# Who issues the transfers of a block inversion: from the SP queue to POOL

## The chip, the cores and the metric

The kernel runs on one core of a Trainium2 chip. The metric is the device time of one execution in microseconds (us), lower is better; it is given as the median of several runs. One further execution is taken with the hardware profiler, and it has a time of its own.

## The reference

One inference step of a two-layer trunk for a prompt of 512 tokens and eight sample tokens with a past of 1024. Layer 0 mixes by a gated DeltaNet, layer 1 by dilated sliding-window attention; each is followed by a squared-ReLU MLP. Everything is float32. What matters here is the prompt's part of the gated DeltaNet: 16 value heads, each evaluated in chunks, where each chunk needs the inverse of a unit lower triangular matrix:

```python
kb = k * beta[..., None]
a_strict = jnp.where(strict, jnp.einsum('bhnid,bhnjd->bhnij', kb, k) * decay, 0.0)
t_inv = lax.linalg.triangular_solve(eye + a_strict, ...,
                                    left_side=True, lower=True, unit_diagonal=True)
u = t_inv @ (v * beta[..., None])
w = t_inv @ (kb * jnp.exp(gc)[..., None])
```

The results are then carried through a scan over the chunks. The outputs are the tokens' new activations, the new states, and the caches with a row appended.

## The kernel before

The program runs four stages one after the other: `gdn` (the gated DeltaNet), `mlp`, `dsw` (the attention) and `mlp` again. Tokens lie along the free dimension (512 of the prompt and 8 samples), features along the 128 partitions. A projection is three float32r matmuls per 128 input features (L164 to L166): weights and activations are split into a high and a low part, ScalarE making the high part (L130) and VectorE the low one (L131). Each weight block comes by a DMA of 512 KB on the SP queue (L145) into one of three buffers, and with each of them goes one copy of old cache rows from DRAM to DRAM (L97).

`gdn` works on eight pairs of value heads, numbered 0 to 7 here. In the loop of L914 the steps of pair p are interleaved with those of pair p + 1, and a scheduler, which lays out the program against a model of its own, decides the order of instructions on each engine from priorities. The order on an engine is fixed then: an engine, the SP queue and POOL each take their instructions strictly one after the other, and one that waits holds back all that stand behind it. For the pair p + 1 the steps are:

- `key`, `decay`: the decay products E (eight tiles u of 128 x 128, four chunks by two heads), made on VectorE, the last of them by L603.
- `invert`: the four 32 x 32 diagonal blocks of each of the eight tiles go out to a DRAM scratch D1 with four transfers (L629, 256 rows of 128 bytes each), and come in again as Ft with one (L632), which puts block (b, u) on partition 32q + 8b + u, four times over. So 32 blocks can be inverted at once by POOL, in 31 steps of two instructions (L638, L641) on a tile Uo; the four copies share out the rows of the result. Uo goes out to the scratch D2 with one transfer (L642, 1024 rows of 128 bytes), and comes in as the diagonal blocks of Uf with four (L646). In the profile both scratches are named D, and Uo and Uf, parts of one tile, are named held.
- `query`, `attend`: the q.k products, multiplied into ET on VectorE (L618) and masked on POOL (L619).
- `merge`: the diagonal blocks are combined to the inverse of the whole 128 x 128 tile. It begins on VectorE with three transposes (L653, L654, L655), which wait for Uf, and on TensorE with L660.
- `values`, `scan`, `gates`, `sample`, `out`, `out_proj`: the rest of a pair. In `sample`, the eight sample states S are brought up to date: a row Du goes to DRAM (L834) and is spread to all partitions as ub (L838), POOL multiplies (L839) and adds (L842), and S goes out (L843). In `out`, a rsqrt (L215 to L221), a scaling of the output (L866) and transposes on TensorE (L871).

`invert` and `merge` run at high priority. All transfers of the program are issued by the SP queue. Where a line below says "SP", it is that queue.

Of the kernel before, what the change touches and what calls it, by code (L numbers as in the profile page):

```python
# [366 lines left out]
def gdn(K, l, done):  # L367


    nc, I, O, tc = K.nc, K.I, K.O, K.tc  # L370
# [5 lines left out]
    with ExitStack() as ctx:  # L376
# [155 lines left out]
        class Pair:  # L532
# [88 lines left out]
            @urgent  # L621
            def invert(self):

                E = self.E
                D1 = K.dp.tile([4, U, 32, 32], F32, tag="D1", name="D1")
                D2 = K.dp.tile([4, U, 32, 32], F32, tag="D2", name="D2")
                for b in range(4):
                    s = slice(32 * b, 32 * b + 32)
                    nc.sync.dma_start(D1[b].rearrange("u i j -> i u j"), E[s, :, s])  # L629

                Ft = K.tile(gp, [P, 32, 32], F32, tag="Ft", name="Ft")
                nc.sync.dma_start(Ft, D1.rearrange("b u i j -> (b u) (i j)")[None].to_broadcast([4, 32, 1024]))  # L632
                Uo = part(f"Uo{self.p % 2}", 32)
                tc.keep_in_program_order(nc.gpsimd.tensor_copy(Uo, eyeU))
                tmp = K.tile(gp, [P, 8, 32], F32, tag="fs", name="fs")
                for j in range(31):
                    n, m = 31 - j, j // 4 + 1
                    nc.gpsimd.tensor_tensor(  # L638
                        tmp[:, :m, :n], Ft[:, None, j + 1 :, j].to_broadcast([P, m, n]), Uo[:, :m, j : j + 1].to_broadcast([P, m, n]), ALU.mult
                    )  # L640
                    nc.gpsimd.tensor_tensor(Uo[:, :m, j + 1 :], Uo[:, :m, j + 1 :], tmp[:, :m, :n], ALU.add)  # L641
                nc.sync.dma_start(D2.rearrange("b u (m q) j -> q (b u) m j", q=4), Uo)  # L642
                Uf = self.Uf = Ufs[self.p % len(Ufs)]
                for b in range(4):
                    s = slice(32 * b, 32 * b + 32)
                    nc.sync.dma_start(Uf[s, :, s], D2[b].rearrange("u m j -> m u j"))  # L646

            @urgent
            def merge(self):
# [761 lines left out]
```

## Time and profile before

| what | value |
| --- | --- |
| median of three runs | 2148.9 us (2146.82 to 2150.51) |
| the profiled execution | 2152.49 us |
| its span, first to last instruction | 2150.7 us |
| its mean granted TensorE clock | 0.954 |
| busy: TensorE, VectorE, ScalarE, POOL | 92%, 61%, 41%, 23% |
| DMA issues of one inversion | 10 (4 + 1 + 1 + 4), 8 inversions |

How to read the lines: PE is TensorE, PEld its weight loads, DVE is VectorE, ACT is ScalarE, POOL is GpSimd, SPq the SP queue. L603 is line 603 of the kernel. `E<-kk,base,ET` names the tile written and the tiles read. A timeline line gives the start in us from the span's start, the duration in us, the engine, the line, the operation and its tiles, how many in a row were merged (x4), and in square brackets how long the engine had been idle before and what ended that. A line of waits gives who waited for whom, the total in us, how often, and the longest. A line of the page's groups gives count, busy us, mean ns of one, and the idle time before. For a DMA issue the time is that of writing the transfer's orders, not that of the data. In the windows view a line gives start and end, length, busy us and instruction count of PE, PEld, DVE, ACT and POOL, the granted TensorE clock, the share of the 16 DMA engines that was busy, and GB/s.

### The profile page before, as it was taken

The page shows a single profiled execution, that of the slowest core. Times are in us where ns is not written, and L with a number is a line of the kernel's source. Part 1 is how long each engine was busy: PE and PEld are TensorE (multiplying, and loading weights), DVE is VectorE, ACT ScalarE, POOL GpSimd, SP SyncE. Part 2 cuts the span into 40 slices and gives each one's busy share as a digit, 9 for nine tenths or more (in the row PEclk, how much of TensorE's full clock was granted, in tenths as well). Part 3 has the DMA queues.
Part 4 walks back from the last instruction along what each step waited for, and adds up shares of the span by engine and source line. Part 5 has one row for each costly group of instructions (what it writes and reads, how often), then busy time and mean ns, then how long its engine had stood idle before and what let it go on. Part 6 is the DMA issues. An engine that isn't in the chain of part 4 may idle for free. (4 is left out here: it accounts for less than half of the span.)

```text
span 2150.7 us, 41729 instructions
## 1 busy us (share of the span) xinstructions
PE 1972.8 (92%) x16436; PEld 1937.4 (90%) x16436; DVE 1319.7 (61%) x3301; ACT 892.5 (41%) x2391; POOL 500.4 (23%) x749
## 2 busy tenths in 40 slices
PE   8959867977968789999999999999999989999998
PEld 7858867977968689999999999999999989999998
DVE  4746766956956575454454667666766784454444
ACT  4525433444434352323244545554555443233231
POOL 1162334444344230000001223322332340000000
PEclk8979988989989789999999999999999999999999
DMA  5534554746844538766765774453454333333332
GB/s 139 101 88 134 145 134 135 225 142 167 250 136 134 190 113 281 253 232 230 251 232 204 240 235 131 119 149 99 119 136 133 114 96 89 98 89 91 97 89 70
DMA packets 416277, 328.55 MB, mean 153 GB/s; under 512 B 48408, under 2 KB 404568, under 8 KB 413896
## 3 DMA queue, kind: packets, MB, share of 16 engines
q1 hardware_dynamic: 416080, 325.88, 50.4%
q8 instruction: 129, 2.11, 0.4%
q14 instruction: 68, 0.56, 0.1%
HBM read 302.19 MB, written 132.83 MB: 202 GB/s over the span
## 5 line engine op out<-in xcount | busy, mean ns | idle before, releaser
L164 PE MATMUL mm<-split,whi 128*128 128x260 f32 (+1 forms) x2960 | 861.7, 291 | 22.0 <-DVE base L848 17.4
L166 PE MATMUL mm<-split,wlo 128*128 128x260 f32 (+1 forms) x2960 | 849.1, 287 | 20.3 <-DVE wlo L131 20.3
L165 PE MATMUL mm<-split,whi 128*128 128x260 f32 (+1 forms) x2960 | 846.5, 286 | 1.1 <-DVE split L178 1.1
L164 PEld LDWEIGHTS mm<-split,whi 128*128 128x128 f32 (+1 forms) x2960 | 564.2, 191 | 24.5 <-DVE base L848 17.5
L166 PEld LDWEIGHTS mm<-split,wlo 128*128 128x128 f32 (+1 forms) x2960 | 563.1, 190 | 23.3 <-DVE wlo L131 22.5
L165 PEld LDWEIGHTS mm<-split,whi 128*128 128x128 f32 (+1 forms) x2960 | 564.3, 191 | 2.1 <-DVE split L178 1.5
L130 ACT CAST whi<-raw 128x1024 fp32r<-128x1024 f32 (+1 forms) x273 | 285.4, 1045 | 503.5 <-PE mm L165 484.2
L131 DVE TENSOR_TENSOR wlo<-raw,whi 128x1024 fp32r<-128x1024 f32 (+1 forms) x273 | 336.5, 1233 | 196.9 <-ACT whi L130 188.0
L166 PE MATMUL mm<-hh,wlo 128*128 128x260 f32 x1024 | 289.1, 283 | 0.0
L165 PE MATMUL mm<-hl,whi 128*128 128x260 f32 x1024 | 288.4, 282 | 0.0
L164 PE MATMUL mm<-hh,whi 128*128 128x260 f32 x1024 | 287.9, 282 | 0.0
L165 PEld LDWEIGHTS mm<-hl,whi 128*128 128x128 f32 x1024 | 192.7, 188 | 0.0
L166 PEld LDWEIGHTS mm<-hh,wlo 128*128 128x128 f32 x1024 | 192.6, 188 | 0.0
L164 PEld LDWEIGHTS mm<-hh,whi 128*128 128x128 f32 x1024 | 192.3, 188 | 0.0
L346 DVE TENSOR_TENSOR t<-mm,bc 128x260 f32<-128x260 f32 x128 | 54.8, 428 | 153.1 <-PE mm L166 153.1
L190 POOL TENSOR_TENSOR acc<-acc,sq 128x260 f32<-128x260 f32 x42 | 37.0, 889 | 380.3 <-ACT sq L189 379.9
L638 POOL TENSOR_TENSOR fs<-Ft,held 128x60 f32<-128x60 f32 (+24 forms) x248 | 90.3, 364 | 112.1 <-DMA Ft<-D 93.4
L130 ACT CAST hh<-q 128x260 fp32r<-128x260 f32 x128 | 52.5, 410 | 121.6 <-DVE q L333 121.6
L641 POOL TENSOR_TENSOR held<-held,fs 128x60 f32<-128x60 f32 (+24 forms) x248 | 90.4, 364 | 19.4
L131 DVE TENSOR_TENSOR hl<-q,hh 128x260 fp32r<-128x260 f32 x128 | 54.9, 429 | 57.1 <-ACT hh L130 57.1
L164 PE MATMUL mm<-onh,whi 128*128 128x260 f32 x256 | 85.2, 336 | 2.8 <-DVE ET L618 2.2
L839 POOL TENSOR_TENSOR ub<-ub,base 128x1024 f32<-128x1024 f32 x16 | 32.7, 2044 | 216.7 <-DMA ub<-Du 201.6
(378 smaller groups left out, 3273.9 us busy)
## 6 DMA issues: line engine op xcount, KB each, us to landing
out_dram<-in_cache_kv_w_dram SPq DMA_DIRECT2D x112, 832.0 KB
raw<-in_dsw_w_in_dram SPq DMA_DIRECT2D x72, 512.0 KB
raw<-in_mlp_w_up_dram SPq DMA_DIRECT2D x64, 512.0 KB
raw<-in_mlp_w_down_dram SPq DMA_DIRECT2D x64, 512.0 KB
raw<-in_gdn_w_in_dram SPq DMA_DIRECT2D x48, 512.0 KB
S<-in_state_gdn_dram SPq DMA_DIRECT2D x16, 512.0 KB
raw<-in_gdn_w_out_dram SPq DMA_DIRECT2D x16, 512.0 KB
ub<-Du SPq DMA_DIRECT2D x16, 512.0 KB
```

The costliest lines, as they stand in the source:

```text
L130: nc.scalar.copy(hi, src)
L131: nc.vector.tensor_tensor(lo, src, hi.bitcast(F32), ALU.subtract)
L164: nc.tensor.matmul(ps[:m], lhsT=w[0][:, k, :m], rhs=xh[:, s], start=k == 0, stop=False)
L165: nc.tensor.matmul(ps[:m], lhsT=w[0][:, k, :m], rhs=xl[:, s], start=False, stop=False)
L166: nc.tensor.matmul(ps[:m], lhsT=w[1][:, k, :m], rhs=xh[:, s], start=False, stop=k == nk - 1)
L190: nc.gpsimd.tensor_tensor(acc[:, s], acc[:, s], t, ALU.add)
L346: nc.vector.tensor_tensor(t, ps, r2[:, s], ALU.mult)
L638: nc.gpsimd.tensor_tensor(tmp[:, :m, :n], Ft[:, None, j + 1 :, j].to_broadcast([P, m, n]), Uo[:, :m, j : j + 1].to_broadcast([P, m, n]), A ...
L641: nc.gpsimd.tensor_tensor(Uo[:, :m, j + 1 :], Uo[:, :m, j + 1 :], tmp[:, :m, :n], ALU.add)
L839: nc.gpsimd.tensor_tensor(ub, ub, kqs[:, :, 0:1].to_broadcast([P, NS, P]), ALU.mult)
```

## The change

Ten `dma_start` calls per inversion (in four statements, two of them in loops of four) go from `nc.sync` to `nc.gpsimd`: POOL writes their orders and they stand in POOL's own order of instructions. Source, target and shape of each stay as they were.

```diff
                 for b in range(4):
                     s = slice(32 * b, 32 * b + 32)
-                    nc.sync.dma_start(D1[b].rearrange("u i j -> i u j"), E[s, :, s])
+                    nc.gpsimd.dma_start(D1[b].rearrange("u i j -> i u j"), E[s, :, s])
...
-                nc.sync.dma_start(Ft, D1.rearrange("b u i j -> (b u) (i j)")[None].to_broadcast([4, 32, 1024]))
+                nc.gpsimd.dma_start(Ft, D1.rearrange("b u i j -> (b u) (i j)")[None].to_broadcast([4, 32, 1024]))
...
-                nc.sync.dma_start(D2.rearrange("b u (m q) j -> q (b u) m j", q=4), Uo)
+                nc.gpsimd.dma_start(D2.rearrange("b u (m q) j -> q (b u) m j", q=4), Uo)
...
                 for b in range(4):
                     s = slice(32 * b, 32 * b + 32)
-                    nc.sync.dma_start(Uf[s, :, s], D2[b].rearrange("u m j -> m u j"))
+                    nc.gpsimd.dma_start(Uf[s, :, s], D2[b].rearrange("u m j -> m u j"))
```

No other line differs, but the scheduler lays out all engines anew. The excerpts of POOL's and VectorE's order, before and after, stand in the prediction beside the terms that rest on them.

## The prediction

> **What bounds the kernel now.** I read the page first, then the waits of TensorE, VectorE and the SP queue, then one inversion in order of time. The page's opening lines, and its slices, where each digit is a fortieth of the span (53.8 us):
>
> ```profile
> span 2150.7 us, 41729 instructions
> PE 1972.8 (92%) x16436; PEld 1937.4 (90%) x16436; DVE 1319.7 (61%) x3301; ACT 892.5 (41%) x2391; POOL 500.4 (23%) x749
> ...
> PE   8959867977968789999999999999999989999998
> ...
> PEclk8979988989989789999999999999999999999999
> ```
>
> TensorE is the bound from slice 15 on; there it is full, and an inversion is not run there. Its holes lie in the first fourteen slices, which is the gated DeltaNet. Who TensorE waited for (columns: total us, times, longest):
>
> ```profile
> PE px L660 <- DMA held<-D: 24.8, 1, 24.8
> PE otr L871 <- DVE osb L866: 22.6, 3, 12.4
> PE mm L166 <- DVE wlo L131: 21.2, 11, 11.4
> PE sut L830 <- DVE base L823: 18.0, 1, 18.0
> PE mm L164 <- DVE base L848: 17.4, 1, 17.4
> PE son L846 <- DVE base L844: 11.6, 1, 11.6
> ```
>
> The first row is an inversion's result coming in. The other five blame five different VectorE instructions, and the longest waits in them (12.4, 11.4, 18.0, 17.4, 11.6) look unrelated. VectorE's own waits tell why they are one thing:
>
> ```profile
> DVE held L653 <- DMA held<-D: 91.0, 7, 19.6
> DVE held L654 <- DMA held<-D: 26.7, 1, 26.7
> ```
>
> VectorE runs in order. Its first instruction of merge (L653) stands in its queue before work that has nothing to do with the inversion, so VectorE stops until the result has landed, 13.0 us in the mean of seven, and TensorE stops a little later for whatever VectorE owes it. The chain that must be followed is thus the inversion's, from the blocks being ready to L653. Here is pair 5 (of 0 to 7), on VectorE, the SP queue, POOL and TensorE:
>
> ```profile
> 486.72 1.12 DVE L603 SCALAR_TENSOR_TENSOR E<-kk,base,ET 128x128 f32<-128x128 f32 x4
> ...
> 535.81 0.43 DVE L653 STREAM_TRANSPOSE held<-held 32x256 f32<-32x256 f32 x1 [14.13 <-DMA held<-D]
> ...
> 540.76 1.22 DVE L866 TENSOR_TENSOR osb<-osb,base 128x1024 f32<-128x1024 f32 x1
> ```
>
> ```profile
> 487.86 1.82 SPq L629 DMA_DIRECT2D D<-E  x4
> ...
> 491.56 0.60 SPq L632 DMA_DIRECT2D Ft<-D  x1
> ...
> 529.33 0.61 SPq L642 DMA_DIRECT2D D<-held  x1
> 534.08 1.80 SPq L646 DMA_DIRECT2D held<-D  x4
> ```
>
> ```profile
> 490.49 1.57 POOL L619 TENSOR_SCALAR_AFFINE_SELECT ET<-ET 128x1024 f32<-128x1024 f32 x1 [9.57 <-DVE base L220]
> 502.69 0.28 POOL L638 TENSOR_TENSOR fs<-Ft,held 128x31 f32<-128x31 f32 x1 [10.64 <-DMA Ft<-D]
> ...
> 529.09 0.22 POOL L641 TENSOR_TENSOR held<-held,fs 128x8 f32<-128x8 f32 x1
> ```
>
> ```profile
> 527.15 0.28 PE L164 MATMUL mm<-split,whi 128*128 128x260 f32 x1
> 527.27 0.28 PE L165 MATMUL mm<-split,whi 128*128 128x260 f32 x1
> 538.93 0.58 PE L166 MATMUL mm<-split,wlo 128*128 128x260 f32 x1 [11.37 <-DVE wlo L131]
> ```
>
> E is ready at 487.84. Blocks out and landed until L632: 3.7 us. Ft in: 11.1. POOL's 31 steps, 502.69 to 529.31: 26.6. Result out and landed (529.33 to 534.08): 4.75. Result in, its first quarter: 1.73. In all 48.0 us, of which TensorE has no work for 11.4. Each us on this chain is a us of the kernel, as long as the hole is there.
>
> **The change, part by part.** It takes ten issues per inversion, 80 in all, from SP and gives them to POOL. What SP gains:
>
> ```profile
> SPq L642 <- POOL held L641: 94.9, 7, 22.2
> ```
>
> SP stood still for 94.9 us before L642, with the next weight loads and the samples' Du and ub behind it. I cost this gain at nothing. The work that hides it is the weight buffers: ScalarE's splits of weights, the first to need a load, wait 484.2 of 503.5 us on TensorE and for no load that the row names outside the MLP:
>
> ```profile
> L130 ACT CAST whi<-raw 128x1024 fp32r<-128x1024 f32 (+1 forms) x273 | 285.4, 1045 | 503.5 <-PE mm L165 484.2 <-ACT sq L189 6.2 <-DMA raw<-in_mlp_w_up_dram 3.9
> ```
>
> If that cover were thinner than I think, this would be a gain on top.
>
> The instructions move as well, since the scheduler orders every engine anew. POOL around the start of pair 5's inversion, before (S_3620 and S_3622 are the previous sample's states):
>
> ```order
> L839 TENSOR_TENSOR ub<-ub,base 128x1024
> L842 TENSOR_TENSOR S_3622<-S_3622,ub 128x1024
> L634 COPY held<-held 128x256
> L619 AFFINE_SELECT ET<-ET 128x1024
> L638 TENSOR_TENSOR fs<-Ft,held 128x31
> ```
>
> and after, from the end of pair 4's inversion (D_3895 is its result, D_4935 pair 5's blocks):
>
> ```order
> L642 DMA D_3895<-held 4x256x32
> L646 DMA held<-D_3895 32x8x32 x4
> L839 TENSOR_TENSOR ub<-ub,base 128x1024
> L842 TENSOR_TENSOR S_3620<-S_3620,ub 128x1024
> L839 TENSOR_TENSOR ub<-ub,base 128x1024
> L842 TENSOR_TENSOR S_3622<-S_3622,ub 128x1024
> L629 DMA D_4935<-E 32x8x32 x4
> L619 AFFINE_SELECT ET<-ET 128x1024
> L632 DMA Ft<-D_4935 128x1x1024
> L634 COPY held<-held 128x256
> L638 TENSOR_TENSOR fs<-Ft,held 128x31
> ```
>
> So the blocks' issue now stands behind the sample's sums, and Ft's issue behind the causal mask of attend. VectorE around pair 5's L653, before (T_6178 is merge's scratch):
>
> ```order
> L848 TENSOR_SCALAR base<-son 128x16
> L653 STREAM_TRANSPOSE held<-held 32x8x32
> L215 TENSOR_SCALAR base<-base 128x24
> L217 TENSOR_SCALAR base<-base 128x24
> L654 STREAM_TRANSPOSE held<-held 32x8x32
> L216 TENSOR_SCALAR base<-base 128x24
> L655 STREAM_TRANSPOSE T_6178<-held 32x256
> L219 TENSOR_TENSOR base<-base 128x24
> L131 TENSOR_TENSOR wlo<-raw,whi 128x1024
> ```
>
> and after:
>
> ```order
> L762 SCALAR_TENSOR_TENSOR sz<-zt,mm 128x260
> L221 SCALAR_TENSOR_TENSOR base<-base 128x24
> L866 TENSOR_TENSOR osb<-osb,base 128x1024
> L877 TENSOR_TENSOR base<-base 128x16
> L653 STREAM_TRANSPOSE held<-held 32x8x32
> L879 SCALAR_TENSOR_TENSOR base<-base,held,sz 128x8 x2
> L654 STREAM_TRANSPOSE held<-held 32x8x32
> L131 TENSOR_TENSOR wlo<-raw,whi 128x1024
> ```
>
> What moved: L653 now stands behind the whole rsqrt, L866, and the weight split for which TensorE waited 11.37 us. Before, that work ran in the trace from just after L653 to L866's end, 536.2 to 542.0, less 0.9 for the two transposes among it: 4.9 us. Counted over the order with the mean duration of each line, VectorE has 5.2 us more to do ahead of L653 in pair 5, and in pairs 2, 3, 4, 6 and 7 it has 5.2, 6.3, 13.0, 3.2 and 3.8 more. In pair 4 I count 9, since its hole is only 11.6. Mean of the six: **5.5 us less stall per pair**, if the chain stayed as long. L660, TensorE's first use of the result, hardly moves in pairs 2 to 7.
>
> Against that stands what POOL's issue costs. The rows nearest to it, from the views of single tiles and lines (ns: min/median/max) and from the page's groups (busy us, mean ns):
>
> ```profile
> L629 SPq DMA_DIRECT2D D<-E x32: 331/448/1578, 86.7 to 652.9; - x32
> ```
>
> ```profile
> L619 POOL TENSOR_SCALAR_AFFINE_SELECT ET<-ET x8: 1093/1331/1948, 93.7 to 654.6; 128x1024 f32<-128x1024 f32 x8
> ```
>
> ```profile
> L839 POOL TENSOR_TENSOR ub<-ub,base 128x1024 f32<-128x1024 f32 x16 | 32.7, 2044 | 216.7 <-DMA ub<-Du 201.6
> ```
>
> No POOL issue is in the trace. From below it is bounded by SP's 0.45 us for the same block (256 rows of 128 bytes), from above by POOL's longest pass over a tile, 2.04. I take s = 1.1 us, an estimate between the 0.45 and the 1.33 of L619, nearer the POOL row, since POOL will have to do the work. For the result out (1024 rows) I take 3s, between one and four blocks.
>
> - Blocks out: 4s = 4.4, then the 1.9 us to land (489.68 to 491.56): 6.3 against 3.7, +2.6. L619 is hidden in the landing: it may start at E + 4.4 and takes 1.33, so ends at E + 5.7. Without that cover it would cost 1.33.
> - Ft: on SP it queues behind bulk loads and cache copies. Alone, in pair 1, it takes 9.2 us, with nothing else at work:
>
> ```profile
> 139.60:148.80 9.20, 0.00 (x0) 0.00 (x0) 0.00 (x0) 0.00 (x0) 0.01 (x1) 0.50 0.26 66
> ```
>
>  A share of 0.26 of 16 engines means about four at work. In a queue of its own: s + 9.2 = 10.3 against 11.1, -0.8.
> - Result out: 3s + 1.9 = 5.2 against 4.75, +0.45.
> - Result in, first quarter: 1.73 - 0.45 + s = 2.4, +0.65.
>
> Sum: the chain is 2.9 us longer. Pairs 2 to 7: 6 x (5.5 - 2.9) = 15.6 us gained. Pair 1 left TensorE no hole, so nothing. Pair 0, the 24.8 us, on POOL and SP:
>
> ```profile
> 93.65 1.95 POOL L619 TENSOR_SCALAR_AFFINE_SELECT ET<-ET 128x1024 f32<-128x1024 f32 x1 [32.56 <-DVE ET L618]
> ...
> 108.30 0.26 POOL L638 TENSOR_TENSOR fs<-Ft,held 128x31 f32<-128x31 f32 x1 [12.35 <-DMA Ft<-D]
> ```
>
> In the new order its Ft is issued behind L619, at 95.6, and lands 10.3 later, at 105.9, which is 2.4 earlier than now. Then POOL issues pair 1's blocks (4.4) and its L619 (1.3) amid pair 0's steps, and the four issues of the result in, all of which L660 needs, take 4.4 where the SP row has 1.8. Together -2.4 + 4.4 + 1.3 + 2.6 = 5.9 later. But in the new order 67 more matmuls stand ahead of pair 0's L660, at 0.12 us each (527.15 to 527.27) 8.0 us of work for TensorE. Gain 2.1. Total **17.7 us**.
>
> The profiled execution took 2152.5 us, span 2150.7; the sum makes it 2134.8. It lies 3.6 above the median of the three runs (2148.9), so for the median I say **2131**.
>
> The Trainium skill, page "DMA: Bandwidth & Descriptors", section "Latency and other measured facts", speaks against the change: it gives about 1 us to the first byte for a transfer whose descriptors GpSimd writes, about 0.6 where hardware writes them, and its issuing table sends simple loads and stores to Sync. By that alone (an estimate) the four hand-offs of a chain would grow by 0.4 us each and the kernel would still gain some 35 us; no run shown here can tell.
>
> **The rivals.**
>
> *POOL's issue is dear* (slower). Each us of s puts 9 us on a chain (4 + 1 + 3 + 1), 54 on six pairs and about 10 on pair 0: 64 per us. The gain is gone at s = 1.38, hardly over the L619 row; at 1.8 the time is 2176, at the upper bound 2.04 it is 2191. For it: POOL's own rows are all dearer than SP's. Against it: it has only addresses to write, no data to pass. To it belongs the wait that the new POOL order can make, blocks behind the sample's L842: L634, which follows L842, started at 480.5 in pair 5, 7.3 us ahead of E (487.84); a sample that comes later than that delays the chain by the rest.
>
> *Ft spreads over all engines* (much faster). The 0.26 above is four engines of 16; on sixteen, the 9.2 us would shrink by 5 or more, the chain would be 2 shorter instead of 2.9 longer, and six pairs gain 30 more: 2101. For it: another generator may divide the rows another way. Against it: the shape is the same, and its four-fold repeat most likely set the four. The same page of the Trainium skill, section "Why a DMA increments its semaphore by 16 and not by 1", has both generators take the largest count up to 16 that divides the outer sizes of both sides, and names an exception for some copies by GpSimd; the 0.26 agrees with the rule.
>
> *A wash.* The later L653 buys nothing because TensorE stops for another VectorE result a little on, and the chain is as long as before: within 4 us of 2149.
>
> **How the numbers follow.** Forecast as worked out 0.45, sixteen engines 0.12, dear issue 0.31, wash 0.12. About 0.2% (4.3 us) is what a measurement here can tell from no change, so faster 0.57, same 0.12, slower 0.31. At s = 0.45 the sum gives about 2100, so the low end, with sixteen engines, is 2095; the high end is s at nearly its bound, 2185. The forecast's own range is 2100 to 2144.
>
> **What would show it.** In the profile after: a POOL queue with 80 issues, the four of L629 taking 4.4 us in all and L642 near 3.3; L638's wait for Ft nearer 10 us; VectorE's wait at L653 about 2.6 us shorter in pairs 2 to 7, holes on TensorE shorter by as much; no wait of SP for L641. It is wrong if the issues take over 1.4 us each, if Ft lands in 5 us, or if TensorE's holes stay while L653's wait shrinks.

## The result, and the profile after

The changed kernel takes 2186.06 us (median of four runs, 2184.3 to 2189.68), the kernel before beside it 2147.95 (2146.82 to 2150.51). The ratio is 1.0178, 95% interval 1.0160 to 1.0196: slower by 1.8%, where 2131 was forecast, and just above the upper end of the range, 2185. The profiled execution took 2184.89 us, span 2183.2. Its page:

```profile
span 2183.2 us, 41786 instructions
...
PE 1980.9 (91%) x16436; PEld 1942.7 (89%) x16436; DVE 1326.0 (61%) x3301; ACT 893.1 (41%) x2391; POOL 573.9 (26%) x829
...
PE   8858969679679679999999999999999989999999
...
PEclk9978789889789689999999999999999999999999
...
q0 software_dynamic: 7424, 7.46, 2.0%
```

TensorE has more low digits in the first fifteen slices, and the rest is as full as before. q0 is the queue that POOL writes. The gated DeltaNet by the windows view, up to its last L871, in the kernel before and then after:

```profile
0.00:762.90 762.90, 615.50 (x5217) 591.22 (x5217) 502.37 (x1472) 317.08 (x913) 283.56 (x577) 0.88 0.53 151
```

```profile
0.00:799.70 799.70, 627.08 (x5222) 599.72 (x5223) 508.00 (x1479) 318.75 (x916) 357.86 (x657) 0.86 0.51 144
```

The stage is 36.8 us longer, and what follows 4.3 shorter. Of the 36.8, TensorE stood idle for 25.2 (799.70 - 627.08 = 172.6, against 147.4) and was busy 11.6 longer with the same matmuls. TensorE's waits now:

```profile
PE px L660 <- DMA held<-D: 56.3, 3, 26.9
PE mm L164 <- ACT onh L130: 17.7, 2, 17.1
...
PE px L660 <- DVE ot L873: 15.4, 1, 15.4
PE mm L164 <- DVE base L896: 12.9, 1, 12.9
PE mm L164 <- DVE sz L762: 12.8, 2, 12.4
```

L660, the first user of an inversion's result, now ends holes itself; before, all long holes but pair 0's ended with something that VectorE owed. VectorE waits longer for the result (117.7 us before, at L653 and L654) although L653 stands later:

```profile
DVE held L653 <- DMA held<-D: 128.6, 8, 26.8
```

Pair 5's inversion after, on VectorE and on POOL, to be read beside the same rows of before:

```profile
504.92 1.37 DVE L603 SCALAR_TENSOR_TENSOR E<-kk,base,ET 128x128 f32<-128x128 f32 x5
...
554.07 1.23 DVE L866 TENSOR_TENSOR osb<-osb,base 128x1024 f32<-128x1024 f32 x1
...
565.08 0.43 DVE L653 STREAM_TRANSPOSE held<-held 32x256 f32<-32x256 f32 x1 [9.70 <-DMA held<-D]
```

```profile
506.58 2.33 POOL L629 DMA_DIRECT2D D<-E  x4 [6.06 <-DVE base L221]
508.92 1.10 POOL L619 TENSOR_SCALAR_AFFINE_SELECT ET<-ET 128x1024 f32<-128x1024 f32 x1
514.60 0.72 POOL L632 DMA_DIRECT2D Ft<-D  x1 [4.57 <-ACT junk L749]
...
526.06 0.25 POOL L638 TENSOR_TENSOR fs<-Ft,held 128x31 f32<-128x31 f32 x1 [9.31 <-DMA Ft<-D]
...
553.27 0.22 POOL L641 TENSOR_TENSOR held<-held,fs 128x8 f32<-128x8 f32 x1
553.79 2.08 POOL L642 DMA_DIRECT2D D<-held  x1 [0.30 <-POOL held L641]
563.12 2.32 POOL L646 DMA_DIRECT2D held<-D  x4 [7.25 <-DMA D<-held]
565.46 1.91 POOL L839 TENSOR_TENSOR ub<-ub,base 128x1024 f32<-128x1024 f32 x1
```

L866 ran ten microseconds ahead of L653, as the new order has it. But the result out took from 553.79 to 563.12, 9.3 us, where SP's took 4.75, and POOL stood still for 7.25 of them, with a sample's L839 behind. The same in all pairs, by the source views of the changed kernel (ns: min/median/max of the issues; below it, us from issue to landing):

```profile
L629 POOL DMA_DIRECT2D D<-E x32: 582/582/794, 85.1 to 681.9; - x32
...
DMA to landing us min/median/max: 1.9/3.5/6.1
```

```profile
L632 POOL DMA_DIRECT2D Ft<-D x8: 717/720/728, 93.7 to 689.1; - x8
...
DMA to landing us min/median/max: 10.2/11.5/14.9
```

```profile
L642 POOL DMA_DIRECT2D D<-held x8: 2057/2082/2090, 147.6 to 729.2; - x8
...
DMA to landing us min/median/max: 8.8/9.2/12.4
```

The issues are cheap; the landing of the result out is slow. In means over pairs 2 to 7, each taken from six rows like the above of the two timelines:

| part of the chain (us) | before | after | change | the prediction's term |
| --- | --- | --- | --- | --- |
| E ready to Ft's issue | 5.6 | 7.6 | +2.0 | +2.6 |
| Ft | 11.1 | 11.7 | +0.6 | -0.8 |
| POOL's 31 steps | 26.6 | 28.2 | +1.6 | none |
| last step to L642 | 0.0 | 0.6 | +0.6 | none |
| result out | 4.8 | 10.2 | +5.4 | +0.45 |
| first L646 to L653 | 2.5 | 2.0 | -0.5 | +0.65 |
| chain, E ready to L653 | 50.7 | 60.4 | +9.7 | +2.9 |

### The profile page after: what moved, and what is told of

The parts are those of the page before. It is cut to its first block, busy times and chain, and to the rows that moved or that the text cites. A ratio compares the mean times of both kernels' runs of the same rounds, so it can differ in the third digit from the quotient of the medians.

```text
span 2183.2 us, 41786 instructions
## 1 busy us (share of the span) xinstructions
PE 1980.9 (91%) x16436; PEld 1942.7 (89%) x16436; DVE 1326.0 (61%) x3301; ACT 893.1 (41%) x2391; POOL 573.9 (26%) x829
## 4 chain that ended last, share of the span: by engine, by line
PE 56%; DVE 8%; DMA 6%; POOL 5%; issue 2%; ACT 2%; SPq 0%; DVEq 0%; POOLq 0%; ACTq 0%
PE mm L166 16%; PE mm L164 16%; PE mm L165 16%; POOL fs L638 2%; DMA Ft<-D 2%; POOL held L641 2%; DMA D<-held 2%; DVE wlo L131 1%; PE po L1218 1%; PE tr L1071 1%; DMA X<-base 1%; PE sco L1138 1%; DVE av L1284 1%; ACT P L1146 1%; DMA base<-X 1%
## 5 line engine op out<-in xcount | busy, mean ns | idle before, releaser
L164 PE MATMUL mm<-split,whi 128*128 128x260 f32 (+1 forms) x2960 | 860.4, 291 | 31.2 <-DVE base L896 12.9
L166 PEld LDWEIGHTS mm<-split,wlo 128*128 128x128 f32 (+1 forms) x2960 | 563.4, 190 | 15.8 <-DVE wlo L131 14.9
L638 POOL TENSOR_TENSOR fs<-Ft,held 128x60 f32<-128x60 f32 (+24 forms) x248 | 98.9, 399 | 101.0 <-DMA Ft<-D 82.2
L641 POOL TENSOR_TENSOR held<-held,fs 128x60 f32<-128x60 f32 (+24 forms) x248 | 95.0, 383 | 19.2
L653 DVE STREAM_TRANSPOSE held<-held 32x256 f32<-32x256 f32 x8 | 3.5, 432 | 128.6 <-DMA held<-D 128.6
```

Of the source, the lines that this page charges most:

```text
L164: nc.tensor.matmul(ps[:m], lhsT=w[0][:, k, :m], rhs=xh[:, s], start=k == 0, stop=False)
L166: nc.tensor.matmul(ps[:m], lhsT=w[1][:, k, :m], rhs=xh[:, s], start=False, stop=k == nk - 1)
L638: nc.gpsimd.tensor_tensor(tmp[:, :m, :n], Ft[:, None, j + 1 :, j].to_broadcast([P, m, n]), Uo[:, :m, j : j + 1].to_broadcast([P, m, n]), A ...
```

## The experiments

Three theories stood against each other. A: the result out moves slowly in POOL's queue. B: POOL's in-order waits delay its other work. C: the new order, with L653 later, costs by itself. Each kernel was compared with the kernel before on its own chip, so the ratios are what to compare. In the table, chain is the mean of pairs 2 to 7 from E ready to L653; cover is the time within it in which TensorE was busy; out is the result out. All three are worked out from the rows of the profiled execution, as in the table above.

| kernel | us | ratio (95%) | chain | cover | out |
| --- | --- | --- | --- | --- | --- |
| before | 2148 | 1 | 50.7 | 38.5 | 4.8 |
| the change | 2186.06 | 1.0178 (1.0160 to 1.0196) | 60.4 | 46.5 | 10.2 |
| e1 only result out | 2180.1 | 1.0142 (1.0117 to 1.0168) | 55.0 | 38.4 | 8.6 |
| e2 all but result out | 2169.42 | 1.0092 (1.0071 to 1.0114) | 56.4 | 45.9 | 5.4 |
| e3 all, result out in four | 2137.04 | 0.9942 (0.9922 to 0.9962) | 56.4 | 47.3 | 6.0 |
| e4 all on SP, Ft in four | 2124.7 | 0.9889 (0.9866 to 0.9911) | 46.0 | 37.8 | 4.9 |
| e5 only Ft | 2149.68 | 1.0016 (1.0005 to 1.0027) | 50.0 | 38.1 | 4.8 |
| e6 all but blocks | 2178.18 | 1.0149 (1.0128 to 1.0171) | 56.4 | 42.6 | 10.6 |
| e7 all on SP, both in four | 2114.72 | 0.9849 (0.9835 to 0.9863) | 45.8 | 38.0 | 4.0 |
| e8 all, both in four | 2099.78 | 0.9775 (0.9762 to 0.9788) | 52.2 | 47.3 | 6.6 |
| e9 only result out, in two | 2198.27 | 1.0229 (1.0210 to 1.0249) | 57.8 | 39.9 | 12.9 |
| e10 only result out, in four | 2137.07 | 0.9943 (0.9925 to 0.9960) | 49.6 | 41.8 | 4.6 |
| e11 all on ScalarE | 2151.28 | 1.0015 (1.0003 to 1.0027) | 48.7 | 38.5 | 5.0 |
| e12 all on ScalarE, both in four | 2128.67 | 0.9904 (0.9885 to 0.9923) | 46.3 | 41.1 | 5.1 |
| e13 only result out, 1 KB rows | 2126.52 | 0.9901 (0.9883 to 0.9918) | 45.9 | 37.5 | 2.1 |
| e14 only result in | 2173.27 | 1.0121 (1.0104 to 1.0138) | 50.7 | 38.9 | 5.3 |
| e15 fours, result in on SP | 2086.73 | 0.9716 (0.9693 to 0.9740) | 50.8 | 47.0 | 5.0 |
| e16 fours, blocks and result in on SP | 2082.94 | 0.9698 (0.9677 to 0.9718) | 46.3 | 42.4 | 4.9 |
| e17 fours, only out on POOL | 2108.7 | 0.9810 (0.9793 to 0.9827) | 45.9 | 41.8 | 5.6 |
| e18 fours, blocks on SP | 2107.46 | 0.9805 (0.9779 to 0.9831) | 51.6 | 46.7 | 7.8 |

"All" means all ten transfers on POOL. The edits stand against the kernel before, or, where said, against the changed one.

**e1, only the result out on POOL.**

```diff
-                nc.sync.dma_start(D2.rearrange("b u (m q) j -> q (b u) m j", q=4), Uo)
+                nc.gpsimd.dma_start(D2.rearrange("b u (m q) j -> q (b u) m j", q=4), Uo)
```

> Only the result out (L642) goes from SP to POOL; the other nine transfers stay on SP. Order of VectorE: L653 has within 0.7 us per pair the same work ahead of it as in the kernel before, so what moves is time on the chain. Theory A (the result out is slow in POOL's queue: 10.25 us from issue to the first L646 in pairs 2 to 7 of the changed kernel, against 4.75): 6 x 5.5 = 33 us more, about 2181, with L653's wait some 5 us longer in each of pairs 2 to 7. Theory B (POOL's in-order waits for the blocks and Ft, L629 and L632, which are not on POOL here): 2148 to 2152. Theory C (the new order, with L653 later, is what costs): 2148, since the order has hardly changed.

Measured 2180.1, as theory A had it. With VectorE's order as before, one transfer of ten makes most of the whole loss. That it came out to the microsecond is partly luck: theory A reckoned with 5.5 us per pair on the chain, and the chain grew by 4.3 (55.0 against 50.7). But the loss lies where the theory puts it. By the two timelines TensorE's idle time in the gated DeltaNet grew by 29.1 us, of which 26.6 lie between E ready and L653 of pairs 2 to 7.

**e2, all but the result out on POOL.** Against the changed kernel:

```diff
-                nc.gpsimd.dma_start(D2.rearrange("b u (m q) j -> q (b u) m j", q=4), Uo)
+                nc.sync.dma_start(D2.rearrange("b u (m q) j -> q (b u) m j", q=4), Uo)
```

> Nine transfers on POOL, the result out (L642) back on SP. Theory A: the chain is 9.7 - 5.5 = 4.2 us longer than before in pairs 2 to 7, of which a later L653 (2.4 us more work ahead of it, counted over the order) takes back 2.4: 6 x 1.8 = 11 us, about 2159. Theory B: nearly all of the loss stays, 2175 to 2190. Theory C (the order costs): L653 is about 40% as much later as in the changed kernel, so about 2163.

Measured 2169.42, above A (2159) and C (about 2163) and below B (2175 to 2190); none of the three had it. So 0.9% remains that is not the result out. e14 takes it up.

**e3, all on POOL, the result out in four; e10, the same four with all else on SP.** Against the changed kernel, and against e1:

```diff
-                nc.gpsimd.dma_start(D2.rearrange("b u (m q) j -> q (b u) m j", q=4), Uo)
+                for q in range(4): nc.gpsimd.dma_start(D2.rearrange("b u (m q) j -> q (b u) m j", q=4)[q], Uo[32 * q : 32 * q + 32])
```

> All on POOL as in the changed kernel, but the result goes out as four transfers of 256 rows (one for each quarter of the partitions) in place of one of 1024. Theory A in the form 'one transfer of 1024 rows runs on four engines': four issues of 0.58 us and 1.9 us to land, 4.2 us in place of 10.25, so 6 x 6 = 36 us less than the changed kernel, about 2150, or less, since L653 stands later still. Theory A in the form 'POOL's queue moves rows of 128 bytes slowly whatever their shape': no shorter than 9 us, 2180 to 2190. Theory B: 2186. Theory C: above 2186, since L653 moves still later (by 1 to 9 us a pair).

> Only the result out on POOL, in four transfers of 256 rows. Work of VectorE from E to L653: 32.6 us (34.0 before), so L653 stands earlier here, unlike in the kernel with all on POOL and the result in four (2137). Result out 4.2 to 6.0 us against 4.75. If the shape of the one transfer was the loss and the rest of the gain there was the later L653: 2149 + 6 x (0.5 + 1.4 x 0.5), 2150 to 2160. If four transfers on POOL are a gain by themselves: 2135 to 2145.

e3: 2137.04, faster than the kernel before, and faster than A's 2150. Theory C falls: of the first four runs this has the latest L653 by the order, and it is faster by 2.3% (by the ratios) than the change of which only L642 was altered. e10 had two forecasts, 2150 to 2160 if only the shape had been the loss and 2135 to 2145 if four transfers on POOL are a gain by themselves; it came in at 2137.07, by the second. The chain is 1.1 us shorter than before, but TensorE also found 3.3 us more work within it (cover 41.8 against 38.5), although the count over VectorE's order had said 1.4 less. That count is no measure of the cover. Nor do chain and cover give the time here: 6 x (1.1 + 3.3) would be 26 us, and 12 were gained.

**e9, only the result out, in two.** Against e1:

```diff
-                nc.gpsimd.dma_start(D2.rearrange("b u (m q) j -> q (b u) m j", q=4), Uo)
+                for q in range(2): nc.gpsimd.dma_start(D2.rearrange("b u (m q) j -> q (b u) m j", q=4)[2 * q : 2 * q + 2], Uo[64 * q : 64 * q + 64])
```

> As the kernel with only the result out on POOL (2180), but the result goes in two transfers of 512 rows. Work of VectorE from E to L653 over the order: 35.9 us (34.0 before). If the time of the one transfer is a matter of how its rows are dealt out to engines (8.7 us for one transfer, 4.2 at best for four), two take about 6: 2149 + 6 x (1.3 - 1.9 x 0.5), about 2151. If POOL's queue costs the same per row: 8.7 stays, 2149 + 6 x (4 - 1), about 2167.

A miss on both sides: 2198.27, worse than the one transfer. Two take 12.9 us, where one took 8.6 and four 4.6.

**e13, only the result out, as 128 rows of 1 KB.** This kernel leaves out the interleaving of the rows: they land in another order than the inverse needs, so its outputs are not the reference's, and it serves for its time alone. Against e1:

```diff
-                nc.gpsimd.dma_start(D2.rearrange("b u (m q) j -> q (b u) m j", q=4), Uo)
+                nc.gpsimd.dma_start(D2.rearrange("b u (x m) j -> (b u x) (m j)", x=4), Uo.rearrange("p m j -> p (m j)"))
```

> Only the result out on POOL, in one transfer over all 128 partitions, but laid out in D2 as 128 rows of 1 KB in the order of the partitions, so that the rows of the inverse land in another order than the reference needs (this part of the computation is changed; all else is as in the kernel with only the result out on POOL, 2180). Order of VectorE as before. If the form with interleaved rows of 128 bytes is what is slow: the result out takes 2 to 4 us in place of 8.7, about 2140 to 2149. If any POOL transfer over all 128 partitions is slow: about 2180.

2126.52, even better than expected (2140 to 2149): the same 128 KB in one POOL transfer over all partitions takes 2.1 us. It isn't POOL, nor the number of partitions; it is the form. The windows view over the result out of one pair, for the kernel before (SP), e1, e9, e10 and e13 in that order; the last three columns are the granted clock, the share of 16 DMA engines and GB/s:

```profile
529.33:534.08 4.75, 0.00 (x0) 0.00 (x0) 0.00 (x0) 0.00 (x0) 0.00 (x0) 0.78 0.19 28
```

```profile
549.99:559.25 9.26, 0.00 (x0) 0.00 (x0) 0.00 (x0) 0.00 (x0) 2.06 (x1) 0.58 0.32 15
```

```profile
562.92:575.96 13.04, 0.00 (x0) 0.00 (x0) 0.00 (x0) 0.00 (x0) 4.11 (x2) 0.61 0.40 12
```

```profile
610.57:614.33 3.76, 0.00 (x0) 0.00 (x0) 0.00 (x0) 0.21 (x1) 2.31 (x4) 0.67 0.23 37
```

```profile
516.90:519.01 2.11, 0.00 (x0) 0.00 (x0) 0.00 (x0) 0.00 (x0) 0.59 (x1) 0.54 0.18 62
```

Length times 16 times share is the engines' time for the same 128 KB: 14.4 us on SP, 47 in one POOL transfer, 83 in two, 13.8 in four, 6.1 as 1 KB rows. The cost of the issue depends on the form too: POOL is busy for 2.06, 4.11, 2.31 and 0.59 us. VectorE did nothing in these five windows and ScalarE next to nothing (0.21 us in e10), so no work of theirs held POOL's transfer up. So a transfer that covers several of the four quarters q, with rows of 128 bytes, costs the DMA engines three to six times as much in POOL's queue as in SP's. A part of that is visible in what the queue moved. POOL's queue in e1, e9, e10 and e13, where it carries the eight results alone (packets, MB, share of 16 engines over the span):

```profile
q0 software_dynamic: 1152, 1.15, 1.0%
```

```profile
q0 software_dynamic: 2304, 1.28, 2.0%
```

```profile
q0 software_dynamic: 1024, 1.05, 0.3%
```

```profile
q0 software_dynamic: 384, 1.05, 0.1%
```

Eight results of 128 KB are 1.05 MB. In one or two transfers the queue moved 0.10 and 0.23 MB more than that. In the packet records these are 96 and 224 further packets of 128 bytes per result, and in the windows above they take 30 of the 47 us and 63 of the 83. What they carry no run shows.

The Trainium skill, page "DMA: Bandwidth & Descriptors", section "Why a DMA increments its semaphore by 16 and not by 1", lets the outermost sizes of both sides set the number of engines, the largest divisor up to 16. By that the outermost sizes here, 4, 2, 32 and 128, give 4, 2, 16 and 16 engines, and the measured 8.6, 12.9, 4.6 and 2.1 us fall in that order. So does Ft (e4). But it does not explain why the same shape, four engines by the same rule, takes half the time on SP; the packets' times overlap in the records, so engines cannot be counted in them. Which of the two, few engines or the further packets, makes how much of the 8.6 stays open.

**e11, all ten issued by ScalarE** (`nc.scalar` in the four statements).

> All ten issued by ScalarE, in the shapes of the changed kernel (result out in one). Work of VectorE from E to L653: 32.0 us (34.0 before). If POOL's queue alone moves the 1024 rows slowly, the result out takes 4.75 us as on SP: about 2149 + 6 x 2 x 0.5, about 2155, and more if ScalarE, which waits for POOL's last step before it can issue L642, keeps weight splits from TensorE. If any queue but SP's is slow: result out near 9, about 2180.

2151.28. The result out takes 5.0 us there, so a queue other than SP's is not slow as such. The issue row of ScalarE's L642 is as cheap as SP's:

```profile
L642 ACTq DMA_DIRECT2D D<-held x8: 518/519/565, 137.9 to 689.0; - x8
```

**e4, all on SP, Ft in four; e7, and the result out in four.**

```diff
-                nc.sync.dma_start(Ft, D1.rearrange("b u i j -> (b u) (i j)")[None].to_broadcast([4, 32, 1024]))
+                for q in range(4): nc.sync.dma_start(Ft[32 * q : 32 * q + 32], D1.rearrange("b u i j -> (b u) i j"))
```

> The kernel before, all on SP, but Ft comes in by four transfers (one for each quarter of the partitions, 32 rows of 4 KB) in place of one of 128. The order of VectorE is the same as before. If four engines of 16 set Ft's time (DMA share 0.26 while nothing else ran), Ft takes about 1.8 + 9.2 / 4 + 1 = 5 us in place of 11.1, and 6 x 6 = 36 us go, and some 4 in pair 0: about 2110. If it is the bulk copies in the engines that set it: 2145 to 2150.

> All on SP; Ft comes in by four transfers, and the result goes out by four. The order of VectorE as before (34 us of work from E to L653). On SP the single result out takes 4.75 us from issue to the first L646; four issues of 0.45 and 1.9 to land would be 3.7: 6 x 1.0 less than with Ft in four alone (2124.7), about 2118. If the single transfer already had enough engines on SP: 2125.

e4: 2124.7. Ft fell from 11.1 to 6.4 us, not to 5, and not quite two thirds of the expected gain came (about 25 of 39 us). So Ft's shape did set much of its time, as few busy engines would have it. POOL's wait for Ft, 93.4 us in eight pairs before, is in e4

```profile
POOL fs L638 <- DMA Ft<-D: 52.2, 8, 7.7
```

e7 took 2114.72 where 2118 was expected: the result out fell to 4.0.

**e5, only Ft on POOL; e6, all but the blocks.** In e5 L632 goes to `nc.gpsimd`; in e6 L629 stays on `nc.sync` and the other three go.

> Only Ft (L632) goes from SP to POOL. The order of VectorE is that of the kernel before, to within 0.5 us per pair. The prediction's term (a queue of its own, free of the bulk loads, 0.8 us a pair shorter): about 2144. Theory A (Ft moves in POOL's queue as on SP, 11.1 to 11.8 us): 2149 to 2153. Theory B (POOL stands at the issue until the blocks have landed and holds back its other work): 2155 or more.

> Ft, result out and result in on POOL, the blocks (L629) back on SP. Here the chain and the order pull apart: the chain should be some 3 us a pair shorter than in the changed kernel (E to Ft's issue 5.65 in place of 7.65, POOL's steps 27 in place of 28.2), but the work of VectorE ahead of L653, counted over the order, falls back from 40.2 us to 33.9 (33.9 is also what the kernel before has: 34.0). If work ahead of L653 is a gain, us for us, as the prediction had it: 6 x (6.3 - 3) = 20 us slower than the changed kernel, about 2200. If it is worth nothing: 6 x 3 = 18 us faster, about 2168; the same if the blocks on POOL are the main loss (theory B).

e5: 2149.68, 0.16% slower, Ft 11.1 us as before. The gain of a queue of its own that the prediction counted is not there. e6: 2178.18, between the two forecasts, and with overlapping intervals not clearly faster than the change. The chain is 4.0 us shorter and the cover 3.9, so they cancel but for little, as a cover that counts us for us should have it; the count over the order had overrated the loss of cover (6.3).

**e14, only the result in on POOL** (L646 to `nc.gpsimd`).

> Only the result in (L646) on POOL. Work of VectorE from E to L653: 33.1 us in pairs 2 to 7 (34.0 before). Each issue 0.58 in place of 0.45, L653 waits for the first: the chain grows by 0.4. By that and the order: 2149 + 6 x (0.4 + 0.9 x 0.5), about 2154. If the part of the loss that stays with the result out on SP sits here: 2158 to 2165.

The second surprise: 2173.27, 1.2% slower, with chain (50.7) and cover (38.9) of pairs 2 to 7 as before. POOL waits for the result to land:

```profile
POOL held L646 <- DMA D<-held: 39.3, 8, 5.4
```

In pair 0 these issues stand in POOL's order among the steps of pair 1, and hold them back:

```profile
148.78 0.25 POOL L638 TENSOR_TENSOR fs<-Ft,held 128x30 f32<-128x30 f32 x1
151.23 2.54 POOL L646 DMA_DIRECT2D held<-D  x4 [2.20 <-DMA D<-held]
153.79 0.25 POOL L641 TENSOR_TENSOR held<-held,fs 128x30 f32<-128x30 f32 x1
```

A step of pair 1 is cut in two, for 4.7 us; its 31 steps take 35.7 us where they took 29.3, and TensorE gets a hole of 6.3 us that was not there, ended by VectorE's L728 after VectorE had stood at pair 1's L653:

```profile
PE pk L713 <- DVE S L728: 6.3, 1, 6.3
```

That is theory B, for a part of the loss. The rest of the loss lies in longer holes in pairs 2 to 7 behind L653, in an order that moved; which wait of POOL's makes them was not settled. The costs of the single transfers don't add up either: 31 us for the result out, 26 for the result in, 3.5 for Ft, against 38 for all ten. In the change the later L653 (cover 46.5) may hide part of them; no run shows that. The blocks were not moved alone.

**e8, all on POOL, both in four; e12, the same on ScalarE.**

> All on POOL; Ft in four and result out in four. Against the kernel with the result alone in four on POOL (2137): Ft some 5 us a pair shorter if its rows of 4 KB gain in POOL's queue as on SP, less 2.6 us of work ahead of L653 lost (38.6 against 41.2): 6 x 2.4 and some 4 in pair 0, about 2119. If POOL's queue gains nothing from four: about 2150.

> All on ScalarE, Ft in four and result out in four. Work of VectorE from E to L653: 30.8 us (34.0 before, 38.6 with the same on POOL). The same on SP took 2114.7, on POOL 2099.8. If the 15 us between those two come from the later L653: ScalarE is above SP, by 6 x 3.2 x 0.5 = 10: about 2125. If they come from SP being free of the inversion's transfers: about 2100 here too.

e8: 2099.78, faster than expected (2119), and by 15 us faster than the same transfers on SP. Its chain is longer than e7's (52.2 against 45.8), but its cover is longer still (47.3 against 38.0). e12 came in at 2128.67, near the 2125 of the theory that the cover makes the difference, and not at the 2100 of SP being free. But that agreement is luck in part. By the windows view of the gated DeltaNet TensorE stood idle for 116.7 us in e7, 91.2 in e8 and 103.0 in e12, so e12's holes are shorter than e7's; what makes its gated DeltaNet longer (741.4 us against 734.1) is TensorE's busy time, 638.4 us against 617.4, and why that grew was not settled. e8's shorter idle time fits the prediction's later L653 as a real gain, when the transfers don't eat it; no run moved the order alone.

**e15 to e18, parts of e8 put back on SP** (the result in; the blocks and the result in; all but the result out; the blocks).

> Blocks, Ft in four and result out in four on POOL, the result in on SP. If POOL's wait for the result's landing costs what the result in alone on POOL cost (26 us): 2099.8 - 26, about 2074. If it costs only its issues and the order (42.1 us of VectorE's work from E to L653 against 38.6): 2099.8 - 6 x (0.6 + 3.5 x 0.5), about 2086. If nothing: 2100.

> Only Ft in four and result out in four on POOL. Against the kernel with the blocks on POOL too, POOL no longer issues blocks between other work: 1 to 3 us a pair less on the chain, but 38.2 us of VectorE's work from E to L653 in place of 42.1. About the same as with the blocks on POOL, 2075 to 2090.

> Only the result out in four on POOL; Ft in four, but on SP. Without Ft in four this took 2137; Ft in four took 24.6 us off the kernel before: about 2112. Order of VectorE as in that kernel (32.6 us).

> As with all on POOL in fours (2099.8), but the blocks on SP. In the changed kernel's shapes taking the blocks back was a gain of 6 us: about 2094. The order of VectorE has 38.6 us from E to L653 here as there.

e15: 2086.73, on the middle one of three forecasts (2074, 2086, 2100). Taking the result in off POOL is a gain of 0.6% here, about half of what e14 would have had it. e16, with 2082.94 the best that was run, is 3.0% faster than the kernel before; against e15 it is the same within the intervals. e17 (2108.7, expected 2112) and e18 (2107.46, expected 2094, a miss) show that taking only the blocks back brings nothing, and, since e16 differs from e17 only in Ft's queue, that Ft on POOL brings 26 us there. Where from is open: chain and cover of e16 and e17 are the same to 0.6 us. VectorE's wait for the result in e16, 117.7 us in the kernel before, has nearly gone:

```profile
DVE held L653 <- DMA held<-D: 29.0, 6, 10.3
DVE held L654 <- DMA held<-D: 4.2, 1, 4.2
```

**Chain, cover and POOL's wait, over all runs.** If chain and cover were all, the gain would be 6 x (growth of the cover - growth of the chain). For the kernels with the result in on POOL, beside POOL's wait at L646 for the landing of the result out (its row in the waits):

| kernel | POOL's wait at L646 (us) | by chain and cover | measured |
| --- | --- | --- | --- |
| e6 | 59.7 | 10 lost | 32 lost |
| the change | 57.0 | 10 lost | 38 lost |
| e2 | 41.3 | 10 gained | 20 lost |
| e14 | 39.3 | 2 gained | 26 lost |
| e3 | 19.7 | 19 gained | 12 gained |
| e18 | 16.0 | 44 gained | 43 gained |
| e8 | 14.8 | 44 gained | 46 gained |

Where POOL stands for 39 us or more, 22 to 30 us are lost beside the chain; where it stands for 20 or less, 7 at most. That fits theory B: the wait costs by what it holds back, and not only by what it adds to the chain. It is a sign and no proof, since the form misses by up to 22 us (e12) among the other kernels, and no run changes this wait alone.

## Why the prediction was wrong

**What bounds the kernel** held. An inversion's chain sets most of the holes in the gated DeltaNet; in e1, e4 and e7, which leave VectorE's order nearly as it was, six times the change of the chain is 26, 28 and 29 us, and the time moved by 31, 25 and 31.

**POOL's issue, 1.1 us estimated**, was too dear: 0.582 per block of 256 rows, near SP's 0.45, and 2.08 for the result out, where 3.3 was taken. What the prediction made the axis of its risk was not the risk. The rival "POOL's issue is dear" gives nearly the measured time (2176 at 1.8 us) for a reason that is false: by its own formula the measured issues would have been a gain. One of the prediction's sums is wrong besides: at 64 us per us of s, s = 0.45 gives 2089 and not 2100, so the range's low end of 2095 is no low end of its own terms.

**Result out, +0.45.** This is the step that failed. It took the landing of the result, 1024 rows, from that of a block, 256 rows (1.9 us), and added only the issue. Its own rows spoke against that: on SP, L642 was issued at 529.33 in 0.61 us, and L646 followed at 534.08, so the same 1024 rows took 4.1 us to land there. On POOL the landing is 9.2 us from the issue's start. Measured +5.4, 32 us over six pairs where the term allowed 3; e1 shows that moving this transfer alone makes the kernel slower by 31.

**Ft, -0.8.** Measured +0.6. The bulk loads ahead of it in SP's queue were not what Ft's time consisted of, and a queue of its own brought nothing (e5). That about four engines set it fits the runs: in four transfers it is 4.7 us shorter (e4). The rival "Ft spreads over all engines" was rightly small: the queue does not change it, the shape does.

**Blocks out, +2.6.** Measured +2.0, in another make-up: the issues are shorter, but Ft's issue comes later. In pair 5 POOL had finished L619 at 510.0, did nothing else, and issued Ft at 514.60. The row lays its wait to ScalarE's L749, which neither reads nor writes Ft or D, so what POOL waited for is not shown.

**POOL's 31 steps** were taken as unchanged. They took 1.6 us more in pairs 2 to 7 and 6.4 more in pair 0 (37.4 against 31.0), where other issues now stand among them. Pair 1 was said to leave no hole; it had one of 6.0, at L713. That POOL waits at L646 for the landing, with its own work behind, was not priced at all; e14 shows 26 us for moving the result in alone, with the chains of pairs 2 to 7 as before. VectorE's wait at L653, which the prediction saw shorter by 2.6 us, grew from 14.6 to 15.8 in the mean of pairs 2 to 7.

**The order's gain, 5.5 us per pair.** Right in kind and too small: TensorE's work within the chain grew by 8.0 us (38.5 to 46.5). The chain grew by 9.7. The prediction's own form, 6 x (order - chain), gives with the measured values 6 x (8.0 - 9.7), 10 us lost, in place of 15.6 gained; the other 28 of the 38 lost lie in neither. The counting over VectorE's order as a measure for it failed in e10.

**Pair 0, 2.1 gained.** Its hole grew from 24.8 to 26.9.

**What was in no term**: TensorE's 11.6 us of longer busy time. A part can be seen in L660, which now starts after holes in pairs 0, 2, 3 and 4; the source view of its tile before and after (ns: min/median/max):

```profile
L660 PE MATMUL px<-held,E x256: 191/191/257, 153.4 to 710.1; 32*32 32x32 f32 x128
```

```profile
L660 PE MATMUL px<-held,E x256: 191/236/258, 161.9 to 745.3; 32*32 32x32 f32 x128
```

The median matmul of L660 takes 236 ns in place of 191. The 32 of pair 4, before and after:

```profile
466.17 1.09 PE L660 MATMUL px<-held,E 32*32 32x32 f32 x32
```

```profile
487.30 2.15 PE L660 MATMUL px<-held,E 32*32 32x32 f32 x32 [12.02 <-DMA held<-D]
```

The granted clock over them was 1.00 before and 0.50 after, and so it is in the other pairs: a mean of 192 ns where it was 1.00, 235 to 237 where it was 0.50. Before, it was 0.50 over L660 in pair 0 alone, behind the hole of 24.8; after, in four pairs, of which three (2, 4 and 7) stand right behind a hole of 12 us or more. So here a hole also cost behind its end. The stage's granted clock fell from 0.88 to 0.86.

The sum: idle 25.2, busy 11.6, later stages -4.3 make the 32.5 by which the span grew. By the two timelines the idle time grew by about 10.6 us between E ready and L653 of pairs 2 to 7, by 5.4 in the same stretch of pairs 0 and 1, and by 11.2 between an L653 and the next pair's E; ahead of the first E it shrank by 1.7. The prediction had no term for the third of these; e1 does not have it (33.9 us there against 34.8 before). SP's freedom was costed at nothing and is not seen: on ScalarE, SP is free too, and the time is the same (e11), with ScalarE's own waits in it.

The Trainium skill, page "DMA: Bandwidth & Descriptors", section "Latency and other measured facts", gives about 1 us to the first byte where GpSimd writes the descriptors, and about 0.6 where hardware does. It spoke against the change with the right sign, but by it the kernel would still have gained, and the traces do not show the difference: from the start of L642's issue to the first packet of the result it is 1.2 us on SP in seven pairs of eight, and 1.2 on POOL in seven pairs of e13 and most of e10; the one transfer of e1 needs 2.7. The size of the loss lies in the shape of one transfer, not in a fixed latency. A block's landing, 3.5 us from the issue's start in the median, is 1.9 at the least.

## What to carry to other kernels

In these runs the landing of a transfer was a property of its shape and queue together: take it from a row of the same shape, and where there is none, bound it by the slowest row, not by the neighbour's. Before a transfer changes its queue, look at its outermost size; the same bytes as four transfers with 32 outermost, or as long rows (a layout that this program could not use as it stands), went from 8.6 to 4.6 and 2.1 us in POOL's queue, and Ft from 11.1 to 6.4 on SP. On an engine that also computes, an issue that must wait for an earlier transfer holds back all that stands behind it; give it to a queue that has nothing else to do, as e15 and e16 do.

## What the runs showed of the hardware that was not expected

- POOL issues a block of 256 rows of 128 bytes in 0.58 us, 128 rows of 1 KB in 0.59, but the result out of 1024 rows in 2.06, and each half of it, 512 rows, in about as much (4.11 for two).
- In POOL's queue the same 128 KB took the DMA engines 6, 14, 47 or 83 us, by form alone; in the two dear forms the queue moved 96 or 224 further packets of 128 bytes per result.
- Splitting a transfer in two made it slower (8.6 to 12.9 us), in four faster (4.6).
- TensorE's matmuls of 32 x 32 took 192 ns at a granted clock of 1.00 and 235 to 237 at 0.50, which stood over L660 in one pair before and in four after.
